# A conformer stage in a new written-out order: one memory key in three pieces, one more convolution block on TensorE for chunk 6

## The chip, the core and the metric

The kernel runs on one core of one Trainium2 chip. The metric is the device time of one execution in microseconds (us); the runs shown below are three executions of the kernel before, and one further execution was recorded by the hardware profiler. The engines are named as the profile names them: PE (TensorE, the matmuls), DVE (VectorE), ACT (ScalarE), POOL (GpSimd) and SP (SyncE, whose queue issues most of the DMAs).

## The reference, cut to what matters

A decoder trunk of two layers over 512 tokens with 1024 channels. Layer 1 opens with a Conformer convolution module, and every layer then runs a cross-attention into 256 memory tokens and a gated MLP. The change lies in the convolution module of layer 1, and in the memory keys and values of layer 1's attention, which the kernel computes in the same stage.

```python
def conformer_conv(x, norm, w1, b1, dw_w, dw_b, ln_g, ln_b, w2, b2):
    h = rms_norm(x, norm) @ w1 + b1          # 1024 -> 2048
    h = jax.nn.glu(h, axis=-1)               # value * sigmoid(gate)
    h = causal_dwconv(h, dw_w, dw_b)         # depthwise, 31 taps
    h = jax.nn.silu(layer_norm(h, ln_g, ln_b))
    return h @ w2 + b2

def cross_attn(x, mem, norm, mem_norm, wq, wk, wv, wo):
    ...
    m = rms_norm(mem, mem_norm)
    k = (m @ wk).reshape(Bn, M, XA_HEADS, XA_HD)
    v = (m @ wv).reshape(Bn, M, XA_HEADS, XA_HD)
    ...
```

## The kernel before, in words

Activations lie with channels on the 128 partitions and tokens along the free axis, so 1024 channels are eight chunks of 128 x 512. All products are done in three matmuls of a split pair (high x high, high x low, low x high): `mm3` issues them on its lines L186, L187 and L188. A weight tile of 128 x 1024 is fetched by SP into `raw` (a ring of three), ACT copies it to its high part `whi` (L166), and the engine `eng` subtracts to get the low part `wlo` (L167). `whi` and `wlo` are rings of four, so the high part of a weight can be written only when PE has finished with the weight four places earlier.

The stage `conformer` first computes the layer's memory keys 0 and 1 (`mem.keys`), around which the token sums of the norm (`token_sums`, L314, four pairs of small matmuls) and its spread over the partitions (`spread`, L350) are placed by the scheduler with priority. Then everything stands in an order written out by hand: inside `tc.manual_schedule` each engine takes its instructions in the order in which the code issues them. `run` reads a string of steps, and a digit behind the letter is the chunk c (a second digit repeats the step):

- `G c`, `V c`: 24 matmuls of 128 x 512, the gate and the value projection of a chunk; `g c` is the sigmoid of the gate on ACT (L1407), `S c` multiplies both on DVE (L1413). For a chunk with `PE_GROUPS` above 0, `S` also sets the first columns of `h` to zero on POOL (L1412) and issues four DMAs from SP that make four shifted copies of `h` (L1420).
- `F`: the next weight is fetched (two places ahead) and the next one is split, ACT the high part and POOL the low part. The order of weights is G0 V0 ... G7 V7 K4 K5 K6 K7 R0 ... R7. R0 to R7 are the pieces of the values' weight; R0 to R3 are split in halves of 512 (`park`).
- `T c`: one tap of the depthwise convolution on DVE, accumulated in PSUM (L1478, the first one L1480). `P c`: one tap on ACT (L1465, L1468), added up by POOL (L1469). `N_POOL` taps of each chunk go that way (5 in chunk 7, otherwise 6).
- `W c` builds block matrices of taps on POOL (L1433), and `C c` runs four taps of every group of `PE_GROUPS[c]` on PE as 32-wide tiles (`conv_pe`, L1443, four matmuls to a group). The taps left over are those of `T`.
- `M c` merges PE's or DVE's sum, POOL's sum and the bias on DVE (L1484) into `outs`, which the layer norm reads; `Q 0` starts its mean over the first four chunks (`quarters`, L298).
- `K n`: 24 matmuls of 128 x 256, a memory key; `k n` and `l n` split it on ACT (L176) and DVE (L181). Keys 0 to 3 have weights that were split in the stage before (`parked`).

Behind the last string the products with R0 to R7 run (`mem.sums`, L458, `go` takes steps of six matmuls), with the parts of the layer norm between them: `quarters(mu, outs, 1)` stands behind the first four of these steps and needs the merges of all chunks.

PSUM has a ring of five tiles for `mm`, two for `aux` and one for `stat`.

Of the kernel before, what the change touches and what calls it, by code (L numbers as in the profile page):

```python
# [20 lines left out]
C = D // P  # L21
# [12 lines left out]
C_RG = 8.0  # L34
TAPS = 31

PE_GROUPS = [0, 0, 0, 4, 0, 0, 4, 6]
N_POOL = [6] * 7 + [5]

KE = 2  # L40
PARKED = 4
# [20 lines left out]
def trunk(ctx: ExitStack, tc: tile.TileContext, I: dict, out: list):  # L62
# [38 lines left out]
    def aux_ps():  # L101
        return aux.tile([P, T], F32, tag="aux", name=nm("aux"))
# [611 lines left out]
    class Seven:  # L714
# [4 lines left out]
        B11, B21, B22, T1, T2, T3, T4 = range(7)  # L719
# [678 lines left out]
    def conformer(norm, nxt, mem, parked):  # L1398
        fold = small.tile([P, 32], F32, tag="fold", name="fold", bufs=1)
        V.tensor_reduce(fold, ident.rearrange("p (a b) -> p a b", b=4), axis=mybir.AxisListType.X, op=ALU.add)  # L1400
        hs, outs = [None] * C, []

        b, psa = [None] * C, [None] * C

# [4 lines left out]
        def gated(c):  # L1409
            h = tmp.tile([P, T + 4], F32, tag="h", name=nm("h"), bufs=4)  # L1410
            if PE_GROUPS[c]:
                G.memset(h[:, :4], 0.0)  # L1412
            V.scalar_tensor_tensor(h[:, 4:], psa[c], col("c_b_pw1", c), b[c], op0=ALU.add, op1=ALU.mult)  # L1413
            stacked = []
            for j in range(4 if PE_GROUPS[c] else 0):
                stacked.append(act_f())
# [10 lines left out]
        def taps_of(c):  # L1427

            n = 4 * PE_GROUPS[c]
            taps[c] = big_f()[:, : n * 32].rearrange("p (a b) -> p a b", b=32)  # L1430
# [51 lines left out]

        def merge(c):
            V.scalar_tensor_tensor(zs[c], accs[c], col("c_dw_b", c), zs[c], op0=ALU.add, op1=ALU.add)  # L1484
            outs.append(zs[c])

        def warm(name, func, ins):
            with tc.issue_after(ins):
# [2 lines left out]
        taps, accs, zs, aside, convs = [[None] * C for _ in range(5)]  # L1491
        names = [k + str(c) for c in range(C) for k in "GV"]
        names += ["K%d" % n for n in range(PARKED, C)] + ["R%d" % n for n in range(READY)]
        raws, ws = [], {}
# [17 lines left out]
        warm("token", AF.Sqrt, norm.square)  # L1512
        for n in range(KE):
            mem.keys(n, parked[n])
            if n == 1:
                with tc.high_priority(URGENT):
                    norm.scale()
# [8 lines left out]
        xs = [None] * C  # L1526
        mem.eng = G
        with tc.manual_schedule(engines=ORDERED | {mybir.EngineType.SP}):
            key2 = mem.products(parked[2], ks=range(4))
            ps0 = project_all([ws["G0"], ws["V0"]], norm.x[:1], last=False)  # L1530
            mem.products(parked[2], key2, range(4, C))
            project_all([ws["G0"], ws["V0"]], norm.x[1:], ps0, 1)
            mu = stat_ps()

            def run(script):
                for step in script.split():
                    k, c, n = step[0], int(step[1:2] or 0), int(step[2:] or 1)
                    if k in "GV":
                        raw[step] = project(ws[step], c, norm.x)
                    elif k == "g":  # L1540
                        sigmoid(c, raw["G%d" % c])
                    elif k == "S":
                        psa[c] = raw["V%d" % c]
                        gated(c)
                    elif k == "T":
                        convs[c] = convs[c] or conv(c)
                        for _ in range(n):
                            next(convs[c])
                    elif k == "P":
                        for _ in range(n):  # L1550
                            next(aside[c])
                    elif k == "M":
                        assert next(convs[c] or conv(c), True) and next(aside[c], True)
                        merge(c)
                    elif k == "F":
                        fetch()
                        weights(G)
                    elif k == "C":
                        conv_pe(c)
                    elif k == "W":  # L1560
                        taps_of(c)
                    elif k == "K":
                        raw[step] = mem.products(ws.get(step, parked[c] if c < PARKED else None))
                    elif k == "k":
                        raw[step] = high(raw["K%d" % c][:, :M], mem.key(c)[0])
                    elif k == "l":
                        low(raw["K%d" % c][:, :M], *mem.key(c))
                    elif k == "Q":
                        quarters(mu, outs, c)

            raw = {"V0": ps0[1], "K2": key2}
            sigmoid(0, ps0[0])
            run("k2 l2 G1 F S0 T0 F T0 P0 T0 P0 T0 P0 T02 V1 g1 T0 F T02 P02 T04 G2 F T0 P0 S1 T0 P1 T1 P1 T0 P1 T1")
            run("T0 T1 K3 F T0 T1 g2 T0 P1 T1 V2 T0 P1 T1 k3 l3 T0 T1 T0 T1 P1 T0 T1 G3 F T0 S2 T1 P2 T0 P2 T1 P2 M0")
            run("T2 P2 T1 V3 F T2 T1 g3 T2 P2 T1 P2 T2 T1 T2 T1 T2 G4 F S3 T1 P3 W3 T2 P3 T1 P3 T2 T1 T2 T1 V4 F T2")
            run("g4 T1 P3 T2 P3 T1 T2 T1 T2 T1 G5 F T2 S4 P3 T1 P4 T2 P4 M1 P4 T4 T2 T4 V5 F T2 T4 g5 T2 P4 T4 P4 T2")
            run("T4 T2 T4 T2 C3 F S5 P4 T4 P5 T2 P5 T4 P5 T2 T4 G6 T2 T3 T2 T3 P5 M2 T4 P5 T3 T4 V6 F T3 g6 T4 P5 T3")
            run("T4 T3 T4 T3 T4 G7 F T3 S6 W6 T4 P6 T3 P6 T4 P6 M3 T5 P6 T4 V7 F T5 T4 g7 T5 P6 T4 P6 T5 T4 T5 T4 T5")
            run("K4 F S7 W7 T4 P7 T5 P7 T4 P7 C6 T5 k4 l4 T4 T5 M4 P7 T5 Q0 T5 P7 T6 K5 T5 T6 T5 F T6 K6 T5 F T6 T5")
            run("k5 l5 T6 C7 T5 k6 l6 T6 F T5 T6 F T5 T6 T5 T6 K7 T5 T7 T5 F T7 F T52 k7 l7 T52 M5 M6 F M7 F")  # L1580
            ready = [ws["R%d" % n] for n in range(READY)]
            ps = [[mm_ps(), mm_ps()] for _ in range(2)]
            mem.eng = None
            steps = (_ for h in range(2) for _ in mem.sums(h, ps[h], ready[4 * h :]))

            def go(n):
                for _ in range(n):
                    next(steps, None)

            go(4)  # L1590
            quarters(mu, outs, 1)
            f = split(mu)
            go(1)
            mean, var, sqs = spread(f, fourths), aux_ps(), []
            for c in range(C):
                V.tensor_tensor(outs[c], outs[c], mean, op=ALU.subtract)
                sqs.append(tmp_f())
                A.activation(sqs[c], outs[c], AF.Square)
                if c == 3:
                    go(3)  # L1600
                    quarters(var, sqs, 0)
            raws = []
            for n in range(2):
                raws.append(wp.tile([P, D], F32, tag="raw", name=nm("raw"), bufs=3))
                nc.sync.dma_start(raws[n], I["pw2"][PAIRED[n]])

            def halves(raw):
                both = [split(raw[:, i : i + T]) for i in (0, T)]
                return [b[0] for b in both], [b[1] for b in both]

            pw = [halves(raws[0])]
            go(1)
            quarters(var, sqs, 1)
            f = tmp_f()
            A.activation(f, var, AF.Copy)
            A.activation(small.tile([P, 1], F32, tag="warm", name="root2", bufs=1), sqs[7][:, :1], AF.Sqrt)
            go(1)
            root = stat_ps()
            for j in range(4):
                PE.matmul(root[:, j : j + 1], f[:, j * P : (j + 1) * P], fourth, start=True, stop=True)  # L1620
            rt = small.tile([P, 4], F32, tag="rtok", name=nm("rtok"), bufs=2)
            A.activation(rt, root[:, :4], AF.Sqrt, bias=eps)
            A.activation(small.tile([P, 1], F32, tag="warm", name="silu", bufs=1), eps, AF.Silu)
            V.reciprocal(rt, rt)
            d = diagonals(rt)
            pw.append(halves(raws[1]))
            go(2)
            r = spread(d)
            go(8)

            def scaled(c):
                if c < C:
                    V.tensor_tensor(outs[c], outs[c], r, op=ALU.mult)

            def silu(c):
                if c < C:
                    A.activation(outs[c], outs[c], AF.Silu, scale=col("c_ln_g", c), bias=col("c_ln_b", c))

            scaled(0)
            silu(0)  # L1640
            scaled(1)
            for c in range(C):
                hi = high(outs[c])
                silu(c + 1)
                scaled(c + 2)
                xs[c] = low(outs[c], hi)
                if c == 0:
                    mem.scaled(0, ps[0])
                elif c == 1:
                    pw.append(load_w(I["pw2"][PAIRED[2]]))  # L1650
                elif c == 5:
                    mem.scaled(1, ps[1])
            mem.eng = None
# [23 lines left out]
    mem = Memory(0, load=False)  # L1677
# [107 lines left out]
    mem, parked = ffn(0, n2, n3, attention(0, n1, mem, n2, six))  # L1785
# [80 lines left out]
```

## Time and profile before

| what | value |
|---|---|
| runs of the kernel before | 1430.33, 1430.71, 1434.24 us; median 1430.71 us |
| the profiled execution | 1431.02 us, of which 1429.2 us from the first to the last instruction |
| mean granted TensorE clock | 0.998 |
| busy share of the span | PE 99%, DVE 83%, ACT 56%, POOL 22% |
| chain of work that ended last | 90% of it PE |
| HBM read | 145.16 MB |

The profile's page gives busy times, the span in 40 slices and the costliest groups of instructions; its trace answers with the waits of an engine (line waited for, us in total, times, longest), the timeline (start in us from the span's start, us taken, engine, line, operation, out<-in, shape, count and in brackets the idle time before it with what ended it), and busy times in stretches. In the timeline matmuls overlap, so the time of one is the distance to the start of the next, not its own length. The stage of the change lies between about 720 and 890 us.

### The profile page before, as it was taken

How to read it: one execution, taken by the hardware profiler on the slowest of the kernel's cores; microseconds unless marked ns; L12 is line 12 of the kernel's file. 1: busy time of each engine (PE TensorE's matmuls, PEld its weight loads, DVE VectorE, ACT ScalarE, POOL GpSimd, SP SyncE). 2: the span in 40 equal slices, each digit the busy share in tenths (PEclk: the TensorE clock that was granted, in tenths of full speed). 3: DMA queues.
4: the chain of work that ended last, by engine and by line, in shares of the span. 5: the costliest groups of instructions: out<-in, count | busy, mean ns of one | idle time of the engine just before them, and what ended most of it. 6: DMA issues, size and time to landing. Idle time of an engine off the chain costs nothing.

```text
span 1429.2 us, 22885 instructions
## 1 busy us (share of the span) xinstructions
PE 1418.0 (99%) x8578; PEld 1259.4 (88%) x8578; DVE 1184.4 (83%) x1980; ACT 800.7 (56%) x1336; POOL 311.2 (22%) x325
## 2 busy tenths in 40 slices
PE   9999999999999999999999999999999999999998
PEld 7988888998899999999988777899889999999997
DVE  6987776778888888888888997978788988888885
ACT  7678754666644444544555547767665444444434
POOL 0011310200122221222008992010012222221201
PEclk9999999999999999999999999999999999999999
DMA  8523232542577777777432454345247876877741
GB/s 302 197 74 104 89 119 80 118 111 89 136 183 169 172 181 165 164 176 169 140 119 89 118 158 153 105 87 148 86 114 162 178 184 157 171 183 159 164 127 60
DMA packets 78591, 202.23 MB, mean 141 GB/s; under 512 B 8848, under 2 KB 9360, under 8 KB 78480
## 3 DMA queue, kind: packets, MB, share of 16 engines
q1 hardware_dynamic: 50544, 150.15, 33.6%
q0 software_dynamic: 27648, 50.34, 21.3%
q8 instruction: 67, 1.10, 0.3%
q14 instruction: 44, 0.36, 0.1%
q10 hardware_dynamic: 288, 0.27, 0.1%
HBM read 145.16 MB, written 2.10 MB: 103 GB/s over the span
## 4 chain that ended last, share of the span: by engine, by line
PE 90%; DVE 3%; DMA 2%; POOL 2%; issue 1%; ACT 1%; SPq 0%; POOLq 0%; DVEq 0%; ACTq 0%
PE mm L187 22%; PE mm L186 22%; PE mm L188 22%; PE aux L186 7%; PE aux L187 7%; PE aux L188 7%; PE mm L458 2%; DMA raw<-in_wv 1%; DVE wlo L167 1%; POOL actf L1469 1%; ACT whi L166 1%; PE aux L531 0%; POOL act L167 0%; POOL tmp L1290 0%; DMA raw<-in_pw 0%
## 5 line engine op out<-in xcount | busy, mean ns | idle before, releaser
L187 PE MATMUL mm<-act,whi 128*128 128x512 f32 (+2 forms) x1077 | 377.1, 350 | 0.6 <-DVE act L181 0.5
L188 PE MATMUL mm<-act,wlo 128*128 128x512 f32 (+2 forms) x1077 | 376.7, 350 | 0.0
L186 PE MATMUL mm<-act,whi 128*128 128x512 f32 (+2 forms) x1077 | 376.6, 351 | 0.0
L187 PEld LDWEIGHTS mm<-act,whi 128*128 128x128 f32 x1077 | 203.7, 189 | 29.0 <-DVE act L167 1.0
L186 PEld LDWEIGHTS mm<-act,whi 128*128 128x128 f32 x1077 | 203.4, 189 | 28.4 <-ACT tmp L1468 0.8
L188 PEld LDWEIGHTS mm<-act,wlo 128*128 128x128 f32 x1077 | 203.6, 189 | 25.8
L797 ACT ACTIVATE bigr<-raw 128x512 fp32r<-128x512 f32 x168 | 105.6, 628 | 166.8 <-DMA raw<-wa 70.4
L188 PE MATMUL mm<-bigr,bigr 128*128 128x256 f32 x672 | 190.2, 283 | 0.0
L187 PE MATMUL mm<-bigr,bigr 128*128 128x256 f32 x672 | 190.2, 283 | 0.0
L186 PE MATMUL mm<-bigr,bigr 128*128 128x256 f32 x672 | 190.0, 283 | 0.0
L171 DVE TENSOR_TENSOR tmp<-mm,tmp 128x256 f32<-128x256 f32 x336 | 136.3, 419 | 31.6 <-PE mm L188 25.9
L186 PE MATMUL aux<-act,whi 128*128 128x512 f32 x399 | 156.3, 392 | 0.0
L187 PE MATMUL aux<-act,whi 128*128 128x512 f32 x399 | 156.2, 391 | 0.0
L188 PE MATMUL aux<-act,wlo 128*128 128x512 f32 x399 | 155.2, 389 | 0.0
L804 DVE TENSOR_TENSOR bigr<-raw,bigr 128x512 fp32r<-128x512 f32 x168 | 115.5, 688 | 37.0 <-ACT bigr L797 34.8
L166 ACT ACTIVATE whi<-raw 128x1024 fp32r<-128x1024 f32 (+1 forms) x95 | 96.4, 1019 | 84.1 <-PE mm L187 44.0
L187 PEld LDWEIGHTS mm<-bigr,bigr 128*128 128x128 f32 x672 | 128.9, 192 | 1.6
L186 PEld LDWEIGHTS mm<-bigr,bigr 128*128 128x128 f32 x672 | 128.9, 192 | 1.5
L188 PEld LDWEIGHTS mm<-bigr,bigr 128*128 128x128 f32 x672 | 128.9, 192 | 0.0
L807 POOL DMA_DIRECT2D raw<-raw x48 | 41.6, 866 | 343.1 <-DVE wlo L804 283.3
L811 POOL DMA_DIRECT2D raw<-wa x48 | 41.5, 864 | 308.3 <-DVE bigr L804 258.5
L167 DVE TENSOR_TENSOR wlo<-raw,whi 128x1024 fp32r<-128x1024 f32 (+1 forms) x75 | 90.5, 1210 | 20.0 <-ACT whi L166 19.8
(351 smaller groups left out, 3026.1 us busy)
## 6 DMA issues: line engine op xcount, KB each, us to landing
raw<-wa POOLq DMA_DIRECT2D x144, 256.0 KB, 4.6
wa<-in_wpair SPq DMA_DIRECT2D x84, 256.0 KB, 3.5
raw<-in_wpair SPq DMA_DIRECT2D x42, 512.0 KB, 5.7
big<-in_wdown SPq DMA_DIRECT2D x42, 512.0 KB, 6.7
raw<-raw POOLq DMA_DIRECT2D x48, 256.0 KB, 7.6
raw<-in_pw SPq DMA_DIRECT2D x24, 512.0 KB, 3.4
raw<-in_win SPq DMA_DIRECT2D x20, 512.0 KB, 3.4
raw<-in_wk SPq DMA_DIRECT2D x16, 512.0 KB, 3.6
```

What stands on the lines that cost most here:

```text
L166: A.activation(hi, src, AF.Copy)
L167: fetched[1] = (eng or V).tensor_tensor(lo, src, hi.bitcast(F32), op=ALU.subtract)
L171: V.tensor_tensor(out, a, b, op=ALU.add)
L186: PE.matmul(ps, wh, xh, start=first, stop=False)
L187: PE.matmul(ps, wh, xl, start=False, stop=False)
L188: PE.matmul(ps, wl, xh, start=False, stop=last)
L458: PE.matmul(p, m[j], x, start=k == 0 and j == 0 and x is hi, stop=k == C - 1 and x is lo)
L797: A.activation(self.w[name][0], self.block(name), AF.Copy)
L804: V.tensor_tensor(lo, self.block(name), hi.bitcast(F32), op=ALU.subtract)
L807: G.dma_start(self.r, self.z, accum_op=ALU.add)
L811: G.dma_start(self.r, self.a22, accum_op=ALU.add)
L1469: G.tensor_tensor(z[:, s:], z[:, s:], f[:, s:], op=ALU.add)
```

## The change

Four things are changed, all in `conformer`. The products of memory key 3 move from the step `K3` of the string to three places: the first two of its eight k-steps behind key 0, the next two at the head of the written-out order ahead of key 2, and the last four at `K3`. For that its PSUM tile comes from the `aux` ring instead of the `mm` ring, which also shifts by one the count by which later projections are dealt to `mm` and `aux`. Chunk 6 gets five groups of taps on PE instead of four, so C6 has 20 matmuls instead of 16 and DVE has four taps less in that chunk. `outs` is filled by index, since merges no longer come in the order of the chunks. The strings of steps are new: the block matrices W6 and W3 come first and W7 in the second string, chunk 7's taps for POOL (P7) stand behind the splits of R0 to R2 on ACT and of R0 to R4 on POOL, key 6 goes ahead of key 5, and C7 follows C6 directly.

```diff
-PE_GROUPS = [0, 0, 0, 4, 0, 0, 4, 6]
+PE_GROUPS = [0, 0, 0, 4, 0, 0, 5, 6]
...
-        hs, outs = [None] * C, []
+        hs, outs = [None] * C, [None] * C
...
-            outs.append(zs[c])
+            outs[c] = zs[c]
...
         for n in range(KE):
             mem.keys(n, parked[n])
+            if n == 0:
+                key3 = mem.products(parked[3], aux_ps(), range(2))
             if n == 1:
...
+            mem.products(parked[3], key3, range(2, 4))
             key2 = mem.products(parked[2], ks=range(4))
...
-                        raw[step] = mem.products(ws.get(step, parked[c] if c < PARKED else None))
+                        raw[step] = mem.products(*((parked[3], key3, range(4, C)) if c == 3 else (ws[step],)))
...
-            run("K4 F S7 W7 T4 P7 T5 P7 T4 P7 C6 T5 k4 l4 T4 T5 M4 P7 T5 Q0 T5 P7 T6 K5 T5 T6 T5 F T6 K6 T5 F T6 T5")
...
+            run("F F T5 T4 T52 T4 T5 l4 T4 F T5 T4 P7 T5 T4 K6 k6 F K5 F C6 P7 T5 k5 T6 P5 T5 l6 T5 T4 T5 T6 C7 P7 T4")
+            run("K7 Q0 P6 l5 P7 M4 T6 T5 P7 T7 F T6 F T5 T6 T5 M6 T7 F M5 M7 k7 l7")
```

On PE, at the end of key 1 in the order before (`mm_1408`; `bigr` are the normed memory tokens, `act_1362` and `act_1363` the high and low part of a parked weight), key 2 (`mm_1440`) follows at once:

```order
L186 MATMUL mm_1408_7811<-bigr_1338_7541,act_1362_7587 128x256
L187 MATMUL mm_1408_7811<-bigr_1339_7542,act_1362_7587 128x256
L188 MATMUL mm_1408_7811<-bigr_1338_7541,act_1363_7588 128x256
L186 MATMUL mm_1440_7912<-bigr_1336_7531,act_1368_7599 128x256
L187 MATMUL mm_1440_7912<-bigr_1337_7532,act_1368_7599 128x256
L188 MATMUL mm_1440_7912<-bigr_1336_7531,act_1369_7600 128x256
```

In the new order PE has two k-steps of key 3 (`aux_1408`, weight `act_1373` and `act_1374`) at this place, of which the second is shown, and only then key 2 (`mm_1441`):

```order
L186 MATMUL aux_1408_7811<-bigr_1336_7531,act_1373_7609 128x256
L187 MATMUL aux_1408_7811<-bigr_1337_7532,act_1373_7609 128x256
L188 MATMUL aux_1408_7811<-bigr_1336_7531,act_1374_7610 128x256
L186 MATMUL mm_1441_7925<-bigr_1336_7531,act_1368_7599 128x256
L187 MATMUL mm_1441_7925<-bigr_1337_7532,act_1368_7599 128x256
L188 MATMUL mm_1441_7925<-bigr_1336_7531,act_1369_7600 128x256
```

So the first gate projection, which follows key 2's first twelve products, comes behind twelve more products of key 3: these six, and six that stand further up behind key 0.

On ACT, near the end of the strings, the order before has the last taps of P7 (`h_1581` is chunk 7) ahead of the halves of R0 (`raw_1571`), R1 (`raw_1578`) and R2 (`raw_1594`); `bigr_1342` is the split of a key:

```order
L1468 ACTIVATE tmp_1589_8826<-h_1581_8804,par_89 128x486
L176 ACTIVATE bigr_1342_7553<-mm_1577_8773 128x256
L1468 ACTIVATE tmp_1591_8852<-h_1581_8804,par_89 128x485
L1468 ACTIVATE tmp_1592_8861<-h_1581_8804,par_89 128x484
L166 ACTIVATE act_1595_8895<-raw_1571_8750 128x512
L166 ACTIVATE act_1597_8899<-raw_1571_8750 128x512
L166 ACTIVATE act_1601_8932<-raw_1578_8798 128x512
L166 ACTIVATE act_1603_8936<-raw_1578_8798 128x512
L176 ACTIVATE bigr_1342_7553<-mm_1593_8865 128x256
L176 ACTIVATE bigr_1342_7553<-mm_1599_8904 128x256
L166 ACTIVATE act_1607_8976<-raw_1594_8893 128x512
L166 ACTIVATE act_1609_8980<-raw_1594_8893 128x512
```

Now, on ACT, the halves of R0, R1 (`raw_1576`) and R2 (`raw_1585`) come first, and only behind R2 stands the first tap of P7 (`h_1580`), with R3 (`raw_1590`) and R4 (`raw_1595`) ahead of the second one:

```order
L176 ACTIVATE bigr_1342_7553<-mm_1579_8769 128x256
L166 ACTIVATE act_1586_8816<-raw_1571_8726 128x512
L166 ACTIVATE act_1588_8820<-raw_1571_8726 128x512
L166 ACTIVATE act_1591_8826<-raw_1576_8763 128x512
L166 ACTIVATE act_1593_8830<-raw_1576_8763 128x512
L166 ACTIVATE act_1596_8844<-raw_1585_8814 128x512
L166 ACTIVATE act_1598_8848<-raw_1585_8814 128x512
L1465 ACTIVATE actf_1600_8854<-h_1580_8795,par_89 128x488
L176 ACTIVATE bigr_1342_7553<-mm_1601_8859 128x256
L166 ACTIVATE act_1603_8887<-raw_1590_8824 128x512
L166 ACTIVATE act_1605_8891<-raw_1590_8824 128x512
L166 ACTIVATE whi_1609_8922<-raw_1595_8842 128x1024
```

So P7 moved behind the fetches of R2, R3 and R4.

On POOL, at the same place, the zeroing of chunk 7's first columns (`h_1581`) is followed before by the block matrix W7, the four additions of P7 (`actf_1587`), and then by the low parts of R0, R1 and R2:

```order
L1412 MEMSET h_1581_8804 128x4
L1433 TENSOR_TENSOR big_1586_8815<-fold_7752,par_89 128x768
L1464 MEMSET actf_1587_8818 128x24
L1469 TENSOR_TENSOR actf_1587_8818<-actf_1587_8818,tmp_1588_8822 128x487
L1469 TENSOR_TENSOR actf_1587_8818<-actf_1587_8818,tmp_1589_8826 128x486
L1469 TENSOR_TENSOR actf_1587_8818<-actf_1587_8818,tmp_1591_8852 128x485
L1469 TENSOR_TENSOR actf_1587_8818<-actf_1587_8818,tmp_1592_8861 128x484
L167 TENSOR_TENSOR act_1596_8896<-raw_1571_8750,act_1595_8895 128x512
L167 TENSOR_TENSOR act_1598_8900<-raw_1571_8750,act_1597_8899 128x512
L167 TENSOR_TENSOR act_1602_8933<-raw_1578_8798,act_1601_8932 128x512
L167 TENSOR_TENSOR act_1604_8937<-raw_1578_8798,act_1603_8936 128x512
L167 TENSOR_TENSOR act_1608_8977<-raw_1594_8893,act_1607_8976 128x512
```

Now, on POOL, the zeroing and the four low parts of R0 and R1 stand just ahead of the rows shown, which begin with R2, and P7's additions (`actf_1600`) come behind R2, R3 and R4, with the last additions of chunks 5 (`actf_1540`) and 6 (`actf_1566`) among them:

```order
L167 TENSOR_TENSOR act_1597_8845<-raw_1585_8814,act_1596_8844 128x512
L167 TENSOR_TENSOR act_1599_8849<-raw_1585_8814,act_1598_8848 128x512
L1464 MEMSET actf_1600_8854 128x24
L167 TENSOR_TENSOR act_1604_8888<-raw_1590_8824,act_1603_8887 128x512
L167 TENSOR_TENSOR act_1606_8892<-raw_1590_8824,act_1605_8891 128x512
L167 TENSOR_TENSOR wlo_1610_8923<-raw_1595_8842,whi_1609_8922 128x1024
L1469 TENSOR_TENSOR actf_1600_8854<-actf_1600_8854,tmp_1612_8947 128x487
L1469 TENSOR_TENSOR actf_1540_8557<-actf_1540_8557,tmp_1613_8953 128x506
L1469 TENSOR_TENSOR actf_1600_8854<-actf_1600_8854,tmp_1615_8987 128x486
L1469 TENSOR_TENSOR actf_1566_8704<-actf_1566_8704,tmp_1617_9020 128x487
L1469 TENSOR_TENSOR actf_1600_8854<-actf_1600_8854,tmp_1618_9024 128x485
L1469 TENSOR_TENSOR actf_1600_8854<-actf_1600_8854,tmp_1619_9030 128x484
```

So the last additions for three merges now stand behind nine low parts and with nothing but R5 to R7 after them. On SP the four copies of chunk 7's `h` come just ahead of the fetch of R2 in both orders.

More of the change, by code (lines that the diff above doesn't have):

```diff
@@ L1572, in conformer @@
             sigmoid(0, ps0[0])
[L1573 to L1578, printed above, removed]
-            run("K4 F S7 W7 T4 P7 T5 P7 T4 P7 C6 T5 k4 l4 T4 T5 M4 P7 T5 Q0 T5 P7 T6 K5 T5 T6 T5 F T6 K6 T5 F T6 T5")
-            run("k5 l5 T6 C7 T5 k6 l6 T6 F T5 T6 F T5 T6 T5 T6 K7 T5 T7 T5 F T7 F T52 k7 l7 T52 M5 M6 F M7 F")
+            run("S0 W6 T03 W3 T0 F T0 F T02 k2 G1 P0 K3 P0 T0 P02 T0 V1 T02 F k3 l3 T02 l2 G2 g1 F T02 S1 T1 P1 T0 P1")
+            run("T1 T0 T12 T0 T1 V2 T0 T1 P0 G3 T0 T1 P1 T0 W7 V3 P1 T1 T0 F P1 T1 P0 T1 T0 G4 T1 g2 T0 S2 T0 M0 T2")
+            run("T1 F P2 T2 P2 T1 P1 g3 T2 T1 T2 F V4 P2 T1 G5 F T2 S3 T2 T1 T2 T1 T2 P2 V5 P3 T1 P2 T2 T1 T2 T1 T2")
+            run("P32 T1 T2 P2 T1 P3 T2 F g4 S4 F T1 P4 T2 T1 T2 C3 T1 M1 T4 T2 P4 F T4 P42 T4 P3 T2 T4 g5 T2 T4 S5 T2")
+            run("P3 T22 T4 T2 P5 T4 T3 P4 T2 T3 P5 G6 T4 T2 V6 T4 T3 T2 F F g6 M2 T5 T4 T3 T4 P5 P4 T3 T4 T5 T3 P5 F")
+            run("T5 G7 S6 P5 P6 T5 P6 T3 g7 T5 T4 T3 P6 T4 P6 T5 T3 F T5 P6 V7 M3 T4 F K4 T5 S7 k4 T5 T4 T52 T4 T5 T4")
+            run("F F T5 T4 T52 T4 T5 l4 T4 F T5 T4 P7 T5 T4 K6 k6 F K5 F C6 P7 T5 k5 T6 P5 T5 l6 T5 T4 T5 T6 C7 P7 T4")
+            run("K7 Q0 P6 l5 P7 M4 T6 T5 P7 T7 F T6 F T5 T6 T5 M6 T7 F M5 M7 k7 l7")
             ready = [ws["R%d" % n] for n in range(READY)]
```

## The prediction

> **What bounds the kernel now.** I read first the page's busy times, then the waits of PE over the whole span, then the busy times in stretches of the convolution stage, and last the timelines around the places that the change touches.
>
> ```profile
> PE 1418.0 (99%) x8578; PEld 1259.4 (88%) x8578; DVE 1184.4 (83%) x1980; ACT 800.7 (56%) x1336; POOL 311.2 (22%) x325
> ...
> PE mm L458 <- ACT whi L166: 1.1, 3, 0.6
> PE stat L139 <- POOL onesf L128: 1.0, 1, 1.0
> PE stat L298 <- DVE actf L1484: 0.8, 1, 0.8
> PE stat L314 <- DVE tmp L248: 0.8, 1, 0.8
> PE mm L187 <- DVE act L181: 0.5, 1, 0.5
> ```
>
> PE is busy for 1418.0 of 1429.2 us, and the waits that the profile names add up to 4.2 us. Three lie in the stage of the change: L314, L187 and L298, 2.1 us together. So nothing that an order does can win more than some 2 us; PE's own work is the kernel. The other engines count only where they make PE wait.
>
> ```profile
> 760.00:780.00 20.00, 20.00 (x101) 17.02 (x101) 19.72 (x31) 11.17 (x16) 19.61 (x16) 1.00 0.38 121
> ...
> 840.00:860.00 20.00, 20.00 (x167) 12.68 (x168) 19.50 (x32) 8.29 (x15) 19.77 (x17) 1.00 0.64 182
> ```
>
> The columns are the stretch, its length, then PE, weight loads, DVE, ACT and POOL in us busy, the granted clock, the DMA share and GB/s. In this stage three engines are full at once: PE 20.00 of 20, DVE 19.50 to 19.72, POOL 19.61 to 19.77. A delay on POOL is hardly made up again before the stage ends, and the layer norm's mean over the last four chunks (`quarters(mu, outs, 1)`, L298, "the second means" below) is where PE meets both.
>
> ```profile
> 735.30 1.05 PE L314 MATMUL stat<-onesf,tmp 128*128 128x1 f32 x8 [0.80 <-DVE tmp L248]
> ...
> 736.54 0.28 PE L186 MATMUL mm<-bigr,act 128*128 128x256 f32 x1
> 736.66 0.28 PE L187 MATMUL mm<-bigr,act 128*128 128x256 f32 x1
> ...
> 741.00 0.39 PE L186 MATMUL mm<-act,whi 128*128 128x512 f32 x1
> 741.92 0.50 PE L187 MATMUL mm<-act,whi 128*128 128x512 f32 x1 [0.52 <-DVE act L181]
> 742.25 0.39 PE L188 MATMUL mm<-act,wlo 128*128 128x512 f32 x1
> 742.48 0.40 PE L186 MATMUL mm<-act,whi 128*128 128x512 f32 x1
> ...
> 811.54 3.60 PE L1443 MATMUL mm<-actf,big 128*32 128x512 f32 x32
> ...
> 864.89 1.06 PE L298 MATMUL stat<-actf,onesf 128*32 128x512 f32 x8 [0.84 <-DVE actf L1484]
> ...
> 741.18 0.69 DVE L181 TENSOR_TENSOR act<-actf,act 128x512 fp32r<-128x512 f32 x1
> ...
> 863.43 1.40 DVE L1484 SCALAR_TENSOR_TENSOR actf<-mm,par,actf 128x512 f32<-128x512 f32 x2
> ```
>
> These rows hold the three waits and their prices. A product of a key starts 0.12 us after the one before (736.54, 736.66), one of a projection 0.23 (742.25, 742.48).
>
> **The change part by part.**
>
> *Key 3 in three pieces.* The number of products stays. What moves is twelve of them (two k-steps behind key 0, two ahead of key 2, three products each), which now run ahead of the first gate projection. The token sums keep their 0.80: in the new order one product of key 3 stands between key 0 and L314, where one product of key 1 stood before. At the first gate projection the second product started 0.92 after the first, and the third 0.33 after that, where a step is 0.23: 0.69 + 0.10 = 0.79 lost. The low part it waited for was written by DVE at 741.18 + 0.69 = 741.87. Twelve products by 0.12 are 1.44, so the projection begins at 742.44, behind that. The 0.79 goes. Next late would be the second token chunk's low part, whose wait PE did not show before and which gets 0.65 us more room. Term: -0.79. The tile taken from the other PSUM ring costs nothing that I can see: before, PE shows no wait for either ring.
>
> *Chunk 6 with a fifth group.* The 32 records of a four-group chunk took 3.60 us, 0.1125 each. Four more matmuls are 8 more records: +0.90 on PE, with nothing beside it, since PE is full. On DVE four taps fall away. Taps that alternate between two chunks start 0.64 us apart:
>
> ```profile
> 816.20 0.73 DVE L1478 SCALAR_TENSOR_TENSOR mm<-h,par,mm 128x490 f32<-128x490 f32 x1
> 816.84 0.72 DVE L1478 SCALAR_TENSOR_TENSOR aux<-h,par,aux 128x482 f32<-128x482 f32 x1
> ```
>
> Four are 2.6 us. That would be worth something only where DVE ends last at the second means. So PE would be ready for the second means at 864.89 - 0.84 - 0.79 + 0.90 = 864.16, against 864.05 before.
>
> *P7 behind R0 to R4.* Here POOL takes DVE's place as the last. The merges of chunks 5, 6 and 7 need POOL's last additions, and in the new order these stand behind the low parts of R0 to R4. I follow the chain from the last place where PE sets its pace, the high part of key 4's weight, which ACT writes when PE has done with the gate weight of chunk 6.
>
> ```profile
> 830.67 3.92 POOL L1469 TENSOR_TENSOR actf<-actf,tmp 128x495 f32<-128x495 f32 x3
> 834.55 2.40 POOL L167 TENSOR_TENSOR wlo<-raw,whi 128x1024 fp32r<-128x1024 f32 x1
> 836.91 2.59 POOL L1469 TENSOR_TENSOR actf<-actf,tmp 128x492 f32<-128x492 f32 x2
> ...
> 841.79 0.11 POOL L1412 MEMSET h<- 128x4 f32 x1
> ...
> 843.35 5.18 POOL L1469 TENSOR_TENSOR actf<-actf,tmp 128x487 f32<-128x487 f32 x4
> 848.49 10.04 POOL L167 TENSOR_TENSOR act<-raw,act 128x512 fp32r<-128x512 f32 x8
> ...
> 820.62 1.06 ACT L166 ACTIVATE whi<-raw 128x1024 fp32r<-128x1024 f32 x1 [4.47 <-PE mm L187]
> ...
> 851.20 1.15 ACT L166 ACTIVATE act<-raw 128x512 fp32r<-128x512 f32 x2 [0.45 <-DMA raw<-in_wv]
> ...
> 841.93 4.20 SPq L1420 DMA_DIRECT2D actf<-h  x4
> 846.22 0.55 SPq L1501 DMA_DIRECT2D raw<-in_wv  x1
> ```
>
> Prices: a low part takes 2.36 (834.55 to 836.91), an addition 1.29 (830.67 to 834.55 by three; 843.35 to 848.49 by four), a half 1.25 (10.04 by eight). Step by step:
>
> 1. Key 4's high part: 820.62 - 0.79 + 1.06 = 820.9.
> 2. From there to the zeroing of chunk 7's columns POOL has four low parts, eight additions and two short memsets: 9.44 + 10.32 + 0.1 = 19.9, so 840.8. Before it was 841.79; the block matrices that now come earlier are not in this stretch.
> 3. SP's four copies started 0.14 after the zeroing, and the fetch of R2, behind them on SP's queue, 4.29 after the first of them: 840.8 + 0.14 + 4.29 = 845.2.
> 4. R2 was there 851.20 - 846.22 = 4.98 after its issue: 850.2. Behind it on ACT's queue wait the first tap of P7 and all that follows.
> 5. POOL has R0 and R1 after the zeroing, four halves, and is through at 845.9. It gets R2's first half at 850.2 + 0.55 + 0.05 = 850.8, an idle time of 4.9 that POOL did not have before, when P7's additions filled this place.
> 6. Then four halves (5.0), R4 (2.36) and six additions (7.74): 865.9. Behind that the last merge, 0.70 + 0.05: 866.65. The second means start at 866.7, against 864.89 before.
>
> PE, ready at 864.16, waits 2.5 us there. Net: 866.7 - 864.89 = **+1.8**. DVE, with four taps less, waits for POOL in its last merges, where before it came last itself. ACT has cover: its work from R2 to the last tap is 0.5 to 1 us an instruction against POOL's 1.25 to 2.36.
>
> Unknown is step 4, as R3 and R4 are now issued right behind R2. The rows give the bounds:
>
> ```profile
> big<-in_wdown SPq DMA_DIRECT2D x42, 512.0 KB, 6.7
> ...
> raw<-in_pw SPq DMA_DIRECT2D x24, 512.0 KB, 3.4
> ...
> raw<-in_wv SPq DMA_DIRECT2D x8, 512.0 KB, 3.9
> ```
>
> The quickest kind of the same size lands after 3.4 (net 1.8 - 1.58 = +0.2), the slowest after 6.7 (+3.5). I take 4.98: it is the same fetch behind the same four copies. That the copies hold up SP's queue is half of the delay: four took 4.20 us to issue, where a plain fetch elsewhere takes 0.33:
>
> ```profile
> 868.85 0.33 SPq L152 DMA_DIRECT2D raw<-in_pw  x1
> ```
>
> [...]
>
> *What lies behind the means.* POOL's low parts of R5 to R7 come later too: R5 at 865.9 + 2.36 = 868.3. PE wants it at
>
> ```profile
> 878.94 0.62 PE L458 MATMUL mm<-wlo,bigr 128*128 128x512 f32 x2
> ```
>
> so there are 10 us of cover, and the delay of the means moves that point back as well. *Key 6 before key 5, C7 behind C6, the filling of outs by index*: the same instructions in other places; C7's copies of `h` are issued by 845.2 and C7 starts near 849 by PE's sum, and what little it might wait there is taken off the wait at the second means. Nothing.
>
> The profiled execution would go from 1431.02 to 1432.8, the median, 0.3 below it, from 1430.71 to **1432.5 us**. About 0.3% (4.3 us) is what a measurement of this kernel can tell from no change, so this is no change by that bound.
>
> **The rivals.**
>
> *A, the forecast*: the second means wait behind R2's fetch, +0.2 to +3.5, likeliest +1.8. For it: the queue of ACT, on which P7 stands behind R2, and 4.98 us from issue to landing in the trace. Chance 0.66.
>
> *B, POOL is in time.* If R2 lands within 2.4 us of step 3's 845.2 (4.9 idle less the 2.5 of PE's wait), POOL's idle time is no longer than the room that it has; at no idle time it ends at 845.9 + 15.1 = 861.0 and PE goes on at 864.16: net 864.16 - 864.89 = -0.7, 1430.0 us. Reasons could be that the copies land and issue faster with less beside them, or that the zeroing comes earlier than I sum. Against it: no kind of fetch lands faster than 3.4. With the near misses up to +0.2, 1430.0 to 1430.9: chance 0.22.
>
> *C, the handoffs slip.* Each of POOL's low parts waits for ACT's high part, and that for PE to have done with the weight four places earlier:
>
> ```profile
> ACT whi L166 <- PE mm L187: 31.9, 12, 4.5
> ```
>
> ACT waited 31.9 us in twelve places for this between 635 and 870. POOL, as full as it is, lost only 0.23 to 0.39 us in each of the two stretches above. If the new strings put a tap that ACT hasn't made, or a high part that PE holds back, in front of POOL x us longer before the zeroing, all of steps 2 to 6 come x later, and the means too: net 1.8 + x. It is slower by over 0.3% from x = 2.5 on, 1435.0 us; at x = 3 it gives 1435.5. For it: the strings are rebuilt from end to end, and POOL has no slack. Against it: 2.5 is ten times what POOL loses in 20 us now. Chance 0.12, of which I give 0.10 to over 0.3%.
>
> [...]
>
> *D, the change fills nothing.* If the gap of 0.79 stayed, since the first projection's inputs also moved, PE would be ready at 864.95 and still wait for POOL to 866.7: the same +1.8 or a little more. It changes the reading, not the time, and lies within A.
>
> **How the numbers follow.** The likeliest is A with 1432.5. The range takes B from a little below its end, 1429.6, and A with its upper bound 1434.2 and a slip of half a us, 1434.8; left out are most of C and the faster tail. Faster by over 0.3% needs 4.3 us where the stage has 2.1 us of waits: 0.02. Slower by over 0.3%: C's 0.10 and 0.02 for A with a late fetch and some slip, 0.12. Same: 0.86.
>
> **What would show it.** Right: the second means on L298 wait about 2.5 us for L1484; DVE's last merges wait for POOL L1469; POOL is idle some 5 us ahead of R2's half (L167) and ACT's L166 there for the DMA of in_wv; the 0.52 at L187 is gone and the 0.80 at L314 is there. L1443 has 120 records for 112. Wrong: no wait at L298 (B), waits of PE for low parts of keys or for copies of `h` before 860 (C), a new wait behind the means, or a wait of the clock below 1.00.

## The result: slower by 0.34%, and the clock pays for the wait

The changed kernel took 1435.86 us in the median of six executions (1434.24 to 1437.62), the kernel before 1430.97 (six executions, 1430.33 to 1434.24): a ratio of 1.0034, 95% interval 1.0024 to 1.0045. A ratio is estimated from all executions of both kernels, so it need not be the quotient of the two medians. The forecast was 1432.5, its range ended at 1434.8. The profiled execution took 1435.82 us, its span 1434.0, 4.8 more than before. One execution of the kernel before that stands beside the first experiments took 1997.27 us at a mean granted clock of 0.655 and is left out of the ratios; the median of 1431.38 given there counts it and would be 1431.32 without it.

First the page's busy times of the changed kernel, then the waits of PE in its trace (line waited for: us in total, times, longest):

```profile
PE 1421.0 (99%) x8586; PEld 1261.6 (88%) x8586; DVE 1182.5 (82%) x1976; ACT 800.5 (56%) x1336; POOL 311.7 (22%) x325
...
PE stat L298 <- DVE actf L1484: 2.4, 1, 2.4
PE mm L458 <- ACT whi L166: 1.2, 2, 1.0
PE stat L139 <- POOL onesf L128: 1.0, 1, 1.0
PE stat L314 <- DVE tmp L248: 0.7, 1, 0.7
PE mm L186 <- ACT act L869: 0.3, 1, 0.3
PE mm L1443 <- DMA actf<-h: 0.2, 1, 0.2
```

The eight records more are the fifth group, four fewer instructions on DVE the taps. The wait at the first projection (L187) is gone, that of the token sums (L314) stands, and the one at the second means (L298) grew from 0.8 to 2.4. PE's busy time is 3.0 us higher, though the added matmuls are worth 0.9: most of the rest is matmuls that ran slower. Where, the busy times in stretches show, in the first row for the kernel before and in the others for the changed kernel (stretch, length, PE, weight loads, DVE, ACT, POOL, granted clock, DMA share, GB/s):

```profile
860.00:880.00 20.00, 19.16 (x97) 13.09 (x96) 12.21 (x22) 13.37 (x22) 8.00 (x4) 1.00 0.59 191
...
840.00:860.00 20.00, 19.84 (x171) 12.02 (x170) 18.41 (x31) 11.09 (x20) 14.63 (x13) 1.00 0.66 202
860.00:880.00 20.00, 17.55 (x80) 11.51 (x78) 12.46 (x20) 9.15 (x15) 13.87 (x9) 0.91 0.47 145
...
865.70:869.10 3.40, 1.32 (x9) 0.45 (x10) 1.92 (x4) 0.19 (x1) 3.37 (x2) 1.00 0.00 0
869.20:872.50 3.30, 3.30 (x9) 2.55 (x8) 0.86 (x2) 0.31 (x1) 3.30 (x3) 0.50 0.47 159
872.60:876.00 3.40, 3.40 (x17) 2.79 (x16) 3.40 (x7) 2.93 (x5) 1.35 (x1) 1.00 0.73 245
```

Right behind the wait, PE ran for 3.4 us at half clock: 9 matmuls in 3.30 us, where the next stretch holds 17 in 3.40. The kernel before has a granted clock of 1.00 in 860 to 880, the changed one 0.91. POOL, full before in 840 to 860 (19.77), now is busy for 14.63 there.

The timeline of the changed kernel, engine by engine, follows the prediction's steps:

```profile
743.28 0.40 PE L186 MATMUL mm<-act,whi 128*128 128x512 f32 x1
743.51 0.40 PE L187 MATMUL mm<-act,whi 128*128 128x512 f32 x1
743.75 0.39 PE L188 MATMUL mm<-act,wlo 128*128 128x512 f32 x1
...
845.74 4.43 PE L1443 MATMUL mm<-actf,big 128*32 128x512 f32 x40
850.34 5.26 PE L1443 MATMUL mm<-actf,big 128*32 128x512 f32 x48 [0.16 <-DMA actf<-h]
...
867.78 1.07 PE L298 MATMUL stat<-actf,onesf 128*32 128x512 f32 x8 [2.44 <-DVE actf L1484]
868.77 2.66 PE L458 MATMUL mm<-act,bigr 128*128 128x512 f32 x6
...
841.72 0.12 POOL L1412 MEMSET h<- 128x4 f32 x1
841.77 5.05 POOL L167 TENSOR_TENSOR act<-raw,act 128x512 fp32r<-128x512 f32 x4
852.19 2.53 POOL L167 TENSOR_TENSOR act<-raw,act 128x512 fp32r<-128x512 f32 x2 [5.37 <-ACT act L166]
...
859.59 7.35 POOL L1469 TENSOR_TENSOR actf<-actf,tmp 128x487 f32<-128x487 f32 x6
866.90 7.05 POOL L167 TENSOR_TENSOR wlo<-raw,whi 128x1024 fp32r<-128x1024 f32 x3
...
841.86 4.24 SPq L1420 DMA_DIRECT2D actf<-h  x4
846.20 13.79 SPq L1501 DMA_DIRECT2D raw<-in_wv  x6
...
851.49 1.15 ACT L166 ACTIVATE act<-raw 128x512 fp32r<-128x512 f32 x2 [8.07 <-DMA raw<-in_wv]
```

The first projection's three products follow each other at 0.23. POOL zeroes chunk 7's columns at 841.72, SP issues the four copies for 4.24 us and asks for R2 at 846.20, ACT gets it at 851.49, POOL stands idle for 5.37 and ends P7's additions at 866.9, and PE starts the second means at 867.78.

Matched instruction by instruction, PE of the changed kernel runs behind that of the kernel before by 0.42 us at 12 us of the span, 0.88 at 714 us, 2.89 at the second means, 4.45 from 872 to 900 us, 4.8 at the end. The 0.42 is there before anything differs. So the profiled difference is 0.4 by chance, 0.46 in the stage before, 2.01 in the stage (2.89 less 0.88), 1.56 for the half clock and 0.3 behind.

### The profile page after: what moved, and what is told of

It is laid out like the page before. It is cut to its first block, busy times and chain, and to the rows that moved or that the text cites. A ratio compares the mean times of both kernels' runs of the same rounds, so it can differ in the third digit from the quotient of the medians.

```text
span 1434.0 us, 22893 instructions
## 1 busy us (share of the span) xinstructions
PE 1421.0 (99%) x8586; PEld 1261.6 (88%) x8586; DVE 1182.5 (82%) x1976; ACT 800.5 (56%) x1336; POOL 311.7 (22%) x325
## 4 chain that ended last, share of the span: by engine, by line
PE 91%; DVE 3%; DMA 2%; ACT 1%; POOL 1%; issue 1%; SPq 0%; POOLq 0%; ACTq 0%; DVEq 0%
PE mm L187 22%; PE mm L186 22%; PE mm L188 22%; PE aux L186 7%; PE aux L187 7%; PE aux L188 7%; PE mm L458 2%; DMA raw<-in_wv 1%; DVE wlo L167 1%; PE aux L531 0%; ACT whi L166 0%; POOL tmp L1290 0%; POOL actf L1469 0%; DMA raw<-in_pw 0%; DVE act L167 0%
## 5 line engine op out<-in xcount | busy, mean ns | idle before, releaser
L187 PE MATMUL mm<-act,whi 128*128 128x512 f32 (+2 forms) x1077 | 377.1, 350 | 0.1
L187 PEld LDWEIGHTS mm<-act,whi 128*128 128x128 f32 x1077 | 203.7, 189 | 28.1 <-DVE act L167 1.0
L187 PE MATMUL mm<-bigr,bigr 128*128 128x256 f32 x672 | 190.2, 283 | 0.0
L187 PE MATMUL aux<-act,whi 128*128 128x512 f32 x399 | 156.2, 392 | 0.0
L187 PEld LDWEIGHTS mm<-bigr,bigr 128*128 128x128 f32 x672 | 128.9, 192 | 1.6
```

The source lines that it names most:

```text
L187: PE.matmul(ps, wh, xl, start=False, stop=False)
```

## The experiments

Medians are given beside the median of the kernel before on the same chip.

**P7 ahead of R2 again.** In the changed kernel's strings, the five steps P7 are put ahead of the F that splits R2:

```diff
-... l4 T4 F T5 T4 P7 T5 T4 K6 k6 F K5 F C6 P7 T5 k5 ... T6 C7 P7 T4  K7 Q0 P6 l5 P7 M4 T6 T5 P7 T7
+... l4 T4 P75 F T5 T4 T5 T4 K6 k6 F K5 F C6 T5 k5 ... T6 C7 T4  K7 Q0 P6 l5 M4 T6 T5 T7
```

Expected: 

> The changed kernel with all five steps of P7 placed ahead of the step that splits R2 and with nothing else moved. Theory 1 (the second means wait 2.44 us because P7's additions stand behind R2's fetch, and this wait lets the clock fall to half for 3.4 us, 1.7 us lost): the wait at L298 goes to 0.3 us or less, the clock stays at 1.00 in the stage, the time falls by 2.4 + 1.7 to about 1431.6 us. Theory 2 (the half clock has nothing to do with that wait): the wait goes, the clock still falls in this stage, about 1433.4 us. Theory 3 (POOL is late anyway, R2 or not): the wait stays over 1.5 us, 1435 us.

Measured: 1431.71 against 1431.38, ratio 1.0005 (0.9996 to 1.0014). The wait at the second means is not among PE's any more, and the stretch of the half clock is at full speed:

```profile
860.00:880.00 20.00, 20.00 (x105) 13.18 (x105) 13.60 (x22) 11.94 (x19) 10.83 (x6) 1.00 0.62 210
```

Beside the kernel before, the loss fell from 4.89 to 0.33 us, so this one place in the order accounts for nearly all of it. Theory 1 fits, 2 and 3 fall. Since the wait and the half clock went together, this run alone does not show that the one brings the other; the four sizes of the wait below do.

**R2 asked for ahead of the copies.** P7 stays behind R2; the fetch alone moves on SP's queue:

```diff
         stacked = []
+        if c == 7:
+            fetch()
         for j in range(4 if PE_GROUPS[c] else 0):
```

Expected: 

> The changed kernel with the fetch of R2 issued ahead of the four copies of chunk 7's h, on the same queue; P7 stays behind R2 on ACT and POOL. Theory 1 (the second means wait because R2 is asked for only after the copies, 4.2 us of issuing, and lands 5 us after that): R2 is there about 4 us earlier, POOL's idle time ahead of its halves falls from 5 us to 1 us or less, the wait at L298 goes, chunk 7's matmuls wait 0.4 to 0.6 us for the copies, about 1432.3 us. Theory 3 (POOL has too much ahead of P7's additions in any case): the wait stays over 1.5 us, 1435 us.

Measured: 1432.88 against 1431.59, ratio 1.0007 (0.9998 to 1.0016). Its timeline, SP, ACT and POOL (two lines were added, so L1503 here is L1501 above and L1422 is L1420):

```profile
841.52 0.33 SPq L1503 DMA_DIRECT2D raw<-in_wv  x1
841.94 4.49 SPq L1422 DMA_DIRECT2D actf<-h  x4
...
845.10 1.15 ACT L166 ACTIVATE act<-raw 128x512 fp32r<-128x512 f32 x2 [1.61 <-DMA raw<-in_wv]
852.13 1.15 ACT L166 ACTIVATE act<-raw 128x512 fp32r<-128x512 f32 x2 [5.02 <-DMA raw<-in_wv]
...
852.84 2.54 POOL L167 TENSOR_TENSOR act<-raw,act 128x512 fp32r<-128x512 f32 x2 [3.77 <-ACT act L166]
```

ACT took R2 up 3.6 us after its issue, 6.4 us earlier than in the changed kernel. But now R3 stands behind the copies, and POOL still idles 3.77, ahead of R3 in the place of R2. With a whole tile's halves done earlier that is enough: PE's wait at the second means fell to 0.2, that for chunk 7's copies rose to 0.9. Theory 3 falls. So the issue of the four copies is a link of the chain, as the prediction had it; the idle time of POOL went less far down than expected.

**More work on PE in the wait.** Ten matmuls that nothing reads, ahead of the second means:

```diff
             go(4)
+            spare = aux_ps()
+            for _ in range(10):
+                PE.matmul(spare, mem.chunk(0, 0, P)[0], blk(ready[0], 0, T)[0], start=True, stop=True)
             quarters(mu, outs, 1)
```

Expected: 

> The changed kernel with ten more matmuls of 128x512 ahead of the second means, whose sum nothing reads (about 2.3 us of PE work in the place of the wait). Theory 1 (the wait sets off the half clock): the means start at the same place, the wait shrinks to about 0.2 us, no half clock behind it, the time falls by 1.7 to about 1434.2 us. Theory 2 (the half clock comes anyway, from the work before or by the time of day): 1435.9 us as the changed kernel, the clock record as there.

Measured: 1435.33 against 1431.38, ratio 1.0029 (1.0018 to 1.0040): half a us below the changed kernel, not 1.7, and within its interval. PE's wait at the second means shrank to 0.5, not to 0.2. The stretches show why this settles little:

```profile
734.30:737.60 3.30, 2.47 (x22) 2.27 (x21) 1.82 (x5) 2.50 (x5) 0.00 (x0) 1.00 0.41 149
737.70:741.00 3.30, 3.30 (x17) 3.20 (x16) 1.60 (x4) 0.00 (x0) 0.00 (x0) 0.50 0.02 6
...
868.40:871.80 3.40, 2.89 (x16) 1.58 (x16) 1.65 (x3) 0.60 (x1) 3.40 (x2) 1.00 0.09 14
871.80:875.20 3.40, 3.40 (x16) 2.82 (x15) 2.96 (x5) 2.21 (x4) 3.40 (x2) 1.00 0.71 254
```

Behind the second means the clock stayed at 1.00, as theory 1 wants, but in this execution it had fallen at 737.7, behind the token sums, where PE waits 0.83 and then runs eight matmuls of one column for 1.05. That the clock can fall there too was not foreseen. The other six executions have no trace.

**The wait alone, in four sizes.** The kernel before, with n more merges of chunk 7 on DVE ahead of the last one (n = 1 to 4):

```diff
+                        if c == 7:
+                            spare = tmp_f()
+                            for _ in range(n):
+                                V.scalar_tensor_tensor(spare, accs[c], col("c_dw_b", c), zs[c], op0=ALU.add, op1=ALU.add)
                         merge(c)
```

Expected of one: 

> The kernel before with one more merge of chunk 7 on DVE ahead of the last one, whose sum nothing reads: 0.66 us more wait of PE at the second means, 1.5 us in all, and no other edit. [...]

Of two: 

> The same with two merges more: a wait of 2.2 us. [...]

Of three: 

> The same with three merges more: a wait of 2.8 us. [...]

Of four: 

> The same with four merges more: a wait of 3.5 us. [...]

The kernel before stood at 1431.41 beside them.

| merges more | wait at L298, us | median, us | less before | time added on DVE in the trace, us | ratio (95% interval) |
|---|---|---|---|---|---|
| 1 | 1.43 | 1431.63 | +0.2 | 0.77 | 0.9999 (0.9990 to 1.0008) |
| 2 | 2.30 | 1434.01 | +2.6 | 1.56 | 1.0013 (1.0005 to 1.0022) |
| 3 | 3.12 | 1436.06 | +4.7 | 2.35 | 1.0030 (1.0020 to 1.0041) |
| 4 | 3.94 | 1435.97 | +4.6 | 3.13 | 1.0029 (1.0018 to 1.0041) |

A merge more took 0.77 to 0.78 us, not the 0.66 expected, so the waits are longer than forecast. A step lies between a wait of 1.43 and one of 2.30, the second means with one merge more and with two:

```profile
865.17 1.06 PE L298 MATMUL stat<-actf,onesf 128*32 128x512 f32 x8 [1.43 <-DVE actf L1484]
...
866.70 1.06 PE L298 MATMUL stat<-actf,onesf 128*32 128x512 f32 x8 [2.30 <-DVE actf L1484]
```

With two merges the eleven executions fall into two heaps: three from 1431.7 to 1432.6, and eight from 1433.5 to 1434.6, some 1.8 us apart; the mean granted clock is 0.999 in the three and 0.997 or 0.998 in the eight. With three and four none is below 1434.4. Five of the 25 executions of the kernel before lie apart as well, at 1433.1 to 1434.0 where the others end at 1432.3. They have no trace, so whether the clock fell in them, behind the token sums for instance, is open. The stretches of the profiled execution with one merge more, the wait and what follows:

```profile
861.00:864.40 3.40, 2.74 (x13) 1.93 (x11) 3.23 (x6) 1.54 (x2) 2.85 (x2) 1.00 0.61 195
864.40:867.80 3.40, 2.63 (x15) 1.51 (x16) 1.41 (x2) 1.18 (x2) 3.40 (x2) 1.00 0.57 190
867.80:871.20 3.40, 3.40 (x17) 2.80 (x16) 2.88 (x5) 2.13 (x4) 0.38 (x1) 1.00 0.80 286
```

with two:

```profile
864.70:868.00 3.30, 1.30 (x9) 0.45 (x10) 1.87 (x3) 1.04 (x2) 3.30 (x2) 1.00 0.53 185
868.10:871.50 3.40, 3.40 (x10) 2.63 (x9) 1.00 (x2) 0.33 (x1) 0.74 (x1) 0.50 0.77 263
```

and with four:

```profile
865.10:868.40 3.30, 0.59 (x8) 0.16 (x8) 2.55 (x4) 0.27 (x1) 3.30 (x2) 1.00 0.43 144
868.50:871.80 3.30, 3.30 (x10) 2.16 (x7) 0.69 (x1) 0.60 (x1) 0.36 (x1) 0.50 0.77 268
```

With nothing changed but these merges, the wait of 2.30 us has a granted clock of 0.50 behind it and the wait of 1.43 has 1.00. The profiled execution with two merges (1434.41) is one of the eight; the others have no trace, so why two merges split the executions is not shown.

**The block matrices later.** W6 and W3 behind the first two steps F:

```diff
-            run("S0 W6 T03 W3 T0 F T0 F T02 k2 ...
+            run("S0 T03 T0 F T0 F W6 W3 T02 k2 ...
```

Expected: 

> The changed kernel with the block matrices W6 and W3 behind the first two weight steps F instead of ahead of them. Theory 1 (POOL builds them in the stage before, at 704 to 708 us, beside DVE, and both run slower there, which reaches PE as a wait of 0.3 us and 0.46 us of offset): DVE's low part there takes 1.22 us again, not 1.76, the time falls by 0.4 to about 1435.4 us, unless the 2.3 us on POOL's queue come out again at the second means, then up to 1437.5. Rival (the 0.46 us is chance between executions): 1435.9 us.

Measured: 1435.82 against 1431.38, ratio 1.0030 (1.0019 to 1.0041), no change from the changed kernel. First the changed kernel's POOL and DVE, then this one's DVE and POOL:

```profile
704.39 3.48 POOL L1433 TENSOR_TENSOR big<-fold,par 128x640 f32<-128x640 f32 x2 [12.83 <-PE mm L187]
705.21 1.76 DVE L167 TENSOR_TENSOR wlo<-raw,whi 128x1024 fp32r<-128x1024 f32 x1
```

```profile
705.96 1.23 DVE L167 TENSOR_TENSOR wlo<-raw,whi 128x1024 fp32r<-128x1024 f32 x1
...
761.80 2.27 POOL L1433 TENSOR_TENSOR big<-fold,par 128x640 f32<-128x640 f32 x2
```

Moving them sets DVE's low part back to 1.23, and PE's wait for L869 (0.3) is gone. The time alone can't tell theory 1 from the rival; the trace shows the mechanism of theory 1, without the gain: PE waits 2.68 at the second means where it waited 2.44. PE, earlier at the means, only waits longer for POOL.

**The edits without the new order.** The changed kernel with the strings of before (four T6 left out, key 3's tile from the `mm` ring).

Expected: 

> The changed kernel with the strings of the kernel before (four taps T6 left out of them, since chunk 6 has five groups on PE; key 3's tile from the mm ring, since the old order holds both aux tiles then). So key 3 in three pieces and the fifth group alone, without the new order. Theory 1 (the two edits on PE are worth -0.79 and +0.90, DVE has 2.6 us less, and the loss is all of the order): no wait at the second means, about 1430.2 us. Rival (the fifth group or the split key cost more than summed): 1431.5 us or more.

Measured: 1431.99 against 1431.38, ratio 1.0005 (0.9996 to 1.0014): no loss clear of the noise, but not theory 1's 1430.2 either, which lies below the interval. By the time the rival's 1431.5 or more fits, but its reason doesn't: in the trace the moved products of key 3 save PE 0.78 and the fifth group costs it 0.83, about as summed. What theory 1 missed is that PE still waits at the second means:

```profile
PE stat L298 <- DVE actf L1484: 0.8, 1, 0.8
```

DVE waits 1.50 us there for ACT's split of key 7 (`k7`) just ahead of the last merges, so four taps less don't let it end earlier.

**Real work in the wait.** The changed kernel with `go(6)` for `go(4)` ahead of the second means.

Expected: 

> The changed kernel with six steps of the products with R0 to R7 ahead of the second means instead of four: 2.7 us of PE's own work in the place of the wait. Theory 1: no wait at the second means, no half clock behind them; at the end of the layer norm two steps fewer hide its chain, so waits of 0.6 to 2 us appear there; about 1433 us. Theory 2 (half clock from another cause): 1434.7 us or more.

Measured: 1434.64 against 1431.59, ratio 1.0021 (1.0012 to 1.0030). The trace has no wait at the second means (the mean granted clock of this execution is 0.999, in the changed kernel's it is 0.998), but two new waits at the end of the layer norm, as theory 1 said:

```profile
PE mm L186 <- ACT whi L166: 0.9, 1, 0.9
...
PE aux L186 <- ACT act L176: 0.5, 1, 0.5
```

So the two steps had been the cover of the layer norm's end. By the median 1.2 us came back (1.8 beside the kernel before: 3.05 of the 4.89 remain), less than the expected 2.9.

**A version that might beat both.** The kernel before with key 3 in three pieces (`mm` ring) and the steps k7 and l7 behind the last merge:

```diff
-... T7 F T52 k7 l7 T52 M5 M6 F M7 F
+... T7 F T52 T52 M5 M6 F M7 F k7 l7
```

Expected: 

> The kernel before with key 3 in three pieces (its tile from the mm ring) and the two halves of key 7's split, k7 and l7, behind the last merge instead of ahead of the merges; groups and strings otherwise as before. In the trace of before DVE waits 1.27 us for k7 just ahead of the last merges. Theory 1: DVE is through 1.6 us earlier, the 0.79 at the first projection and the 0.84 at the second means both go, about 1429.8 us. Rival (what goes there comes back as a wait further on, at the layer norm's end or in the attention): 1431.4 us as before.

Measured: 1431.22 against 1431.59, ratio 1.0000 (0.9991 to 1.0009). The second means no longer wait. Matched with the kernel before, PE gains 1.1 us from the token sums to the second means and loses half of it at once, at the next step (L350, a wait of 0.2 by the profile), which needs the split of these means on DVE. No version here is measurably faster than the kernel before.

## Why the prediction was wrong

- *Key 3 in three pieces, -0.79:* right. The three products of the first projection start at 743.28, 743.51 and 743.75, and L314 keeps its wait (0.71). Just after the token sums PE runs 0.84 us later than in the kernel before, and 0.05 later once the moved products are made up.
- *Fifth group, +0.90:* 4.43 for 40 records against 3.60 for 32, +0.83.
- *The chain of P7, steps 1 to 6:* right in mechanism and size. Less the 0.88 us that the execution was behind already: zeroing 840.84 (forecast 840.8), R2 asked for 845.3 (845.2), R2 on ACT 850.6 (850.2; ACT took it up 5.29 after its issue, not 4.98), POOL idle 5.37 (4.9), second means 866.9 (866.7), PE's wait 2.44 (2.5), net in the stage +2.0 (+1.8). The two experiments on P7 and on the fetch confirm both links.
- *What failed: no term for the clock.* The forecast priced the wait of 2.5 us of the likeliest case, A, at its own length. The trace of the kernel before could not price it higher: PE's longest wait there is 1.0 us, and the stage is at a granted clock of 1.00. The changed kernel's trace shows 0.50 behind 2.44 us, and the four sizes of the wait show it behind 2.30. So the term of +1.56 us was missing from A, and it is what put the time above the range (1434.3 without it, the range ends at 1434.8). One piece of 3.41 us at 0.50, half of which is 1.7, cost PE 1.56 here and 1.56 to 1.58 with two, three and four merges more. The prediction had listed "a wait of the clock below 1.00" among its signs of being wrong, and that sign came.
- *A small term left out:* step 2's "the block matrices that now come earlier are not in this stretch" looked only at the stretch. They ran in the stage before, beside DVE, and set PE back there by 0.46 us. The wait at the second means hides that in this order, as moving them showed.
- *A bound misread, without effect:* "no kind of fetch lands faster than 3.4" holds for the rows shown there; the full list of the kernel before has three more kinds of 512 KB (`in_wo`, `in_wout`, `in_wq`) with a median of 3.3.
- *Rival B's ground, that without the wait the change gains 0.7:* not borne out: the kernel with P7 ahead is at +0.3 (ratio 1.0005, 0.9996 to 1.0014).
- The direction was right. "Same" by 0.3% was missed narrowly: 0.34%, with an interval from 0.24 to 0.45%; a third of it is the clock. Of the 3.36 us between forecast and median, 1.56 are the clock, 0.46 the block matrices, 0.2 the later means, 0.3 lie behind the stage, and 0.26 the kernel before itself (1430.97 in six executions, 1430.71 in the three of the forecast); for the remaining 0.6 no cause was found.

## What to carry to other kernels

Look at the granted clock behind a wait of PE before pricing it: in the traces here, waits of 2.30, 2.44, 3.12 and 3.94 us at the second means cost 1.56 to 1.58 us more than their length, and one of 1.43 cost no more than itself. When steps go behind a split of a fetched tile, follow the tile's fetch back on its queue: four copies ahead of it, 4.24 us of issuing here, delayed everything behind the split. A wait filled at one place comes back where the filler had been the cover (0.9 and 0.5 us with six steps for four), so look for the next wait before counting a gain.

## What the runs showed of the hardware

The granted clock, as the traces record it: in the changed kernel 1.00 from 5.54 us of the span for 863.57 us, 0.50 for 3.41, 1.00 for 559.79 and 0.50 from 1432.31 on; in the kernel before 1.00 from 4.46 us for 1419.94 us and 0.50 from 1424.40 on. The three stretches at 1.00 are 253.0, 164.0 and 416.0 times the 3.413 us of the one at 0.50 that lies inside the kernel.

What lay ahead of a clock of 0.50, in the stretches shown above: around the second means PE was busy for 0.59 of 3.30 us (four merges more), 1.30 of 3.30 (two merges) and 1.32 of 3.40 (changed kernel), and 0.50 followed each. With ten matmuls ahead of the means it was busy for 2.89 of 3.40, and 1.00 followed. Behind the token sums of that same execution 0.50 followed 2.47 of 3.30, where eight matmuls of one column took 1.05. The length of the wait alone does not sort these cases: 0.50 followed 0.83 us of waiting at the token sums, and 1.00 followed 1.43 us at the second means (one merge more). No run shows what decides between them, and none varies the matmuls of one column.

POOL's block matrices and DVE's low part were slower side by side: two block matrices took 3.48 us beside the low part (changed kernel, 704.39) and 2.27 in the next stage (block matrices later, 761.80), and the low part took 1.76 us beside them (changed kernel, 705.21) against 1.23 without (block matrices later, 705.96).
